# A two-layer RG-LRU and gated-DeltaNet trunk: one-step scaling of the decays, and further margins in the generator that writes the instruction order

## The chip, the cores and the metric

The kernel runs on one core of one Trainium2 chip. The metric is the device time of one launch in microseconds (us). A launch takes the host's arrays and returns the output; nothing is computed on the host.

The core has five engines that run side by side, each through its own list of instructions in the written order: TensorE (PE in the profile; PEld is its loading of weights), VectorE (DVE), ScalarE (ACT), GpSimd (POOL) and SyncE (SP). SyncE here only issues DMA transfers. An instruction that waits for a result holds everything behind it on its engine.

## The reference

The input x has 2048 frames of 1024 channels, all in float32. Layer 0 mixes with a recurrent block (RG-LRU), layer 1 with a gated delta rule (DeltaNet) of 8 heads of 128.

```python
c_act = jax.nn.silu(c)
for i in range(2):
    shift, scale, gate = split(c_act @ ada_w[i] + ada_b[i])
    h = rmsnorm(x, norm_g[i]) * (1.0 + scale) + shift
    out = rglru_block(h, ...) if i == 0 else gated_deltanet_block(h, ...)
    x = x + gate * out
return rmsnorm(x, final_g)

# rglru_block: proj = h @ in_w (1024 -> 2048); causal conv of width 4; two gates per 128-wide block;
#   h_t = a_t h_{t-1} + b_t over all frames; times SiLU(z); @ out_w (1024 -> 1024)
# gated_deltanet_block: proj = h @ in_w (1024 -> 4096 + 16); causal conv and SiLU on q, k, v; l2norm of q, k;
#   per head, in chunks:
#     S_t = a_t S_{t-1} + beta_t k_t (v_t - a_t S_{t-1}^T k_t)^T,   o_t = S_t^T q_t
#   rmsnorm per head, times SiLU(z), @ out_w (1024 -> 1024)
```

## The kernel before

The frames are taken in two halves of 1024 (`u`), each in two pieces of 512 (`i`). The program runs through these stages: projections of layer 0 for u = 0 and 1 ("in1"), the output projection of layer 0 ("out1"), projections and heads of layer 1 for u = 0 and 1 ("in2"), the output projection of layer 1 with the last norm ("out2"). Every large product is done as three matmuls in a reduced float32 format, hi x hi, hi x lo and lo x hi, so each weight and each activation is split: ScalarE or VectorE makes the hi copy, and VectorE or GpSimd subtracts it to get lo. Such a 128x512 product is line L668 in the profile; its tile is `mm` in the projections and `mmo` in the output projections.

For layer 1, each of the 32 column panels of a half (k, v, q and z of 8 heads) has its weights split as it comes: `whi` by ScalarE (L644) and `wlo` by GpSimd (L650, 128x1024). In the second half `wlo` is loaded back from memory and GpSimd doesn't compute it again. A k, v or q panel goes through `conv2_thread`: a copy, three taps on VectorE (L718), a tanh on ScalarE (`tt`, L1009), and a product on VectorE (`kt`, `vt`, `qt`, L1014).

Per head and piece, `key_thread` makes the decay matrix `ec` (128 x 4 x 128: four blocks of 128 frames), gets `cc` (one number per row and block) from GpSimd, scales `ec` by it (L1162), and multiplies it with k k^T (`ac`). `inverses_thread` inverts the 32x32 corners in 31 steps on VectorE (`ttmp`, `tblk`, L1293 and L1296); `levels_thread` builds the inverse of 128x128 from them (`px`, `pr`). `recurrence_thread` then takes eight blocks in a row: `pp` (state times k and q, TensorE), `zt` (VectorE, L1422), `py` (TensorE), `yt` (ScalarE, L1436), `pS` (TensorE), the new `state` (VectorE, L1455). `output_thread` adds the two parts of the output and takes its square (`junko`).

No order is written by hand. The functions are generators ("threads"), and at build time a planner, `Weave`, runs them in a model time. A thread yields what it needs next: `"act", 0.53` is 0.53 us on ScalarE (an optional third number is the delay until others see the result), `"none", 0.5` is a pause that occupies no engine, an `Event` is a result of another thread, and `Slots` are the buffers of a ring. The planner always resumes the thread that can start first, and the code behind the yield then emits its instructions. So the model times set the order in each engine's list; they issue nothing. Waits between engines come from the data.

Two rings matter here. `raw` has two buffers of 4 KB per partition; the weight panels, the `ada_w` pieces, the pieces of the output weights (`oraw`) and the first eight rows `ot` of the last norm share it. `xr` has two buffers, shared by the lo parts `xl` of the gates in layer 0 and the residual pieces of out1.

In `out_weights_thread` the output weights come in pieces of 512 KB (L896); `out_split_thread` makes their `oh` (ScalarE, L907) and `ol` (VectorE, L909). The residual pieces are loaded in L970 and stored in L959, the product of the layer goes out in L849, and the kept lo weights in L658.

## Time and profile before

| | |
|---|---|
| median of 3 runs | 1942.98 us (1942.18 to 1945.73) |
| profiled execution | 1942.17 us, its span 1940.5 us, mean TensorE clock 0.984 |
| instructions in the profile | 31373 |
| TensorE matmuls in the profile | 10286, busy 1846.8 us |
| VectorE, ScalarE, GpSimd busy | 1479.8, 1045.5, 647.4 us |
| memory traffic | 322.77 MB, mean 166 GB/s |

All durations in the text come from that one profiled execution. A row of a group of instructions has the line, the engine, the operation, the tiles written and read, the shapes and the count, and then the busy time in us, the mean of one in ns, and the idle time of the engine just before them with what ended it. A row for a line's spread has minimum, median and maximum in ns. A row of the chain of waits has who waited for whom, the total in us, the count and the longest. A row of a timeline has the start and the duration in us; in brackets stands the idle time before it. A row of windows has, for each engine, the busy time and the count, and then the granted TensorE clock (1.00 is full), the DMA share and GB/s.

### The profile page before, as it was taken

The numbers are of one execution on the slowest core, as the hardware profiler recorded it, in microseconds if no ns is written. First come the engines' busy times: TensorE is split into PE (matmuls) and PEld (weight loads), VectorE is DVE, ScalarE is ACT, GpSimd is POOL, SyncE is SP. The second block draws the span as 40 slices with busy tenths as digits, with TensorE's granted clock in tenths as the row PEclk, the third lists the DMA queues.
The fourth block names the chain that finished last, engine by engine and source line by source line (L and its number), as shares of the span: only waits on it lengthen the run. The fifth ranks groups of instructions, "written<-read, shape, count | busy, mean of one in ns | idle before, by whom it ended". The sixth has DMA issues, their size and how long they took to land.

```text
span 1940.5 us, 31373 instructions
## 1 busy us (share of the span) xinstructions
PE 1846.8 (95%) x10286; PEld 1505.6 (78%) x10286; DVE 1479.8 (76%) x3271; ACT 1045.5 (54%) x2587; POOL 647.4 (33%) x1116
## 2 busy tenths in 40 slices
PE   6999899999899998998999999999999999999998
PEld 3787678878687777787777777787888888888887
DVE  6899998887454668869878987668787878886653
ACT  3766667667211345475565654565766656655221
POOL 3345542223100244345435532333333223301110
PEclk9999999999899999999999999999999999999999
DMA  8476746554578634556676645556465555586751
GB/s 319 114 221 190 225 140 220 182 161 139 168 209 223 206 110 136 139 136 159 156 180 156 141 119 168 144 136 169 105 159 152 149 127 144 143 233 201 246 160 66
DMA packets 511724, 322.77 MB, mean 166 GB/s; under 512 B 371268, under 2 KB 439236, under 8 KB 511560
## 3 DMA queue, kind: packets, MB, share of 16 engines
q1 hardware_dynamic: 511560, 320.77, 58.7%
q8 instruction: 81, 1.33, 0.3%
q14 instruction: 83, 0.68, 0.1%
HBM read 219.93 MB, written 100.73 MB: 165 GB/s over the span
## 4 chain that ended last, share of the span: by engine, by line
PE 51%; DVE 22%; DMA 10%; ACT 6%; issue 4%; SPq 4%; POOL 2%; DVEq 0%; POOLq 0%; ACTq 0%
PE mm L668 25%; PE mmo L668 15%; DVE xf L718 4%; DVE ttmp L1293 2%; DVE tblk L1296 2%; PE pg L807 2%; DMA blk<-blk_d 1%; DMA raw<-in_w 1%; DMA ada<-in_ada_w 1%; DVE xf L756 1%; PE pp L1413 1%; PE pS L1442 1%; PE py L1430 1%; PE pS L1443 1%; ACT junk L1146 1%
## 5 line engine op out<-in xcount | busy, mean ns | idle before, releaser
L718 DVE SCALAR_TENSOR_TENSOR xf<-xe,cw_s,xf 128x512 f32<-128x512 f32 x288 | 231.0, 806 | 20.3 <-POOL xf L997 16.3
L650 POOL TENSOR_TENSOR wlo<-raw,whi 128x1024 fp32r<-128x1024 f32 x48 | 119.4, 2487 | 141.6 <-ACT whi L644 132.1
L1293 DVE TENSOR_TENSOR ttmp<-blk,tblk 128x60 f32<-128x60 f32 (+24 forms) x496 | 122.4, 247 | 15.7 <-DMA blk<-blk_d 6.6
L644 ACT CAST whi<-raw 128x1024 fp32r<-128x1024 f32 x96 | 100.0, 1042 | 59.1 <-DMA raw<-in_w 51.9
L1296 DVE TENSOR_TENSOR tblk<-tblk,ttmp 128x60 f32<-128x60 f32 (+24 forms) x496 | 121.8, 246 | 10.4 <-DVE ttmp L1293 0.9
L668 PE MATMUL mmo<-oh,yh 128*128 128x512 f32 x256 | 102.1, 399 | 5.0 <-ACT oh L907 5.0
L668 PE MATMUL mm<-hh_('in2', 0)_5342,whi 128*128 128x512 f32 x256 | 105.6, 413 | 0.8 <-ACT xe L730 0.8
L668 PE MATMUL mm<-hh_('in2', 0)_5437,wlo 128*128 128x512 f32 x256 | 105.3, 411 | 0.0
L668 PE MATMUL mmo<-ol,yh 128*128 128x512 f32 x256 | 102.4, 400 | 3.0 <-DVE ol L909 3.0
L668 PE MATMUL mm<-hh_('in2', 1)_12057,whi 128*128 128x512 f32 x256 | 104.9, 410 | 0.0
L668 PE MATMUL mm<-hl_('in2', 0)_5438,whi 128*128 128x512 f32 x256 | 104.9, 410 | 0.0
L668 PE MATMUL mm<-hh_('in2', 0)_5437,whi 128*128 128x512 f32 x256 | 104.7, 409 | 0.0
L668 PE MATMUL mm<-hh_('in2', 1)_12057,wlo 128*128 128x512 f32 x256 | 104.5, 408 | 0.0
L668 PE MATMUL mm<-hl_('in2', 0)_5343,whi 128*128 128x512 f32 x256 | 104.1, 407 | 0.0
L668 PE MATMUL mm<-hl_('in2', 1)_12307,whi 128*128 128x512 f32 x256 | 103.9, 406 | 0.0
L668 PE MATMUL mm<-hh_('in2', 0)_5342,wlo 128*128 128x512 f32 x256 | 103.7, 405 | 0.0
L668 PE MATMUL mm<-hh_('in2', 1)_12306,wlo 128*128 128x512 f32 x256 | 103.5, 404 | 0.0
L668 PE MATMUL mm<-hl_('in2', 1)_12058,whi 128*128 128x512 f32 x256 | 103.5, 404 | 0.0
L668 PE MATMUL mm<-hh_('in2', 1)_12306,whi 128*128 128x512 f32 x256 | 103.4, 404 | 0.0
L668 PE MATMUL mmo<-ol,oh 128*128 128x512 f32 (+1 forms) x264 | 103.0, 390 | 0.0
L668 PE MATMUL mmo<-oh,ol 128*128 128x512 f32 (+1 forms) x264 | 102.9, 390 | 0.0
L668 PE MATMUL mmo<-oh,yl 128*128 128x512 f32 x256 | 102.1, 399 | 0.5 <-DVE yl L929 0.5
(331 smaller groups left out, 5651.9 us busy)
## 6 DMA issues: line engine op xcount, KB each, us to landing
raw<-in_w SPq DMA_DIRECT2D x96, 512.0 KB, 4.2
araw<-in_ada_w SPq DMA_DIRECT2D x32, 512.0 KB, 4.2
xt<-x_d SPq DMA_DIRECT2D x32, 512.0 KB, 4.7
xt_d<-xb SPq DMA_DIRECT2D x192, 64.0 KB, 2.4
xk<-xt_d SPq DMA_DIRECT2D x24, 512.0 KB, 6.2
xt<-in_x SPq DMA_DIRECT2D x16, 512.0 KB, 4.5
ada<-in_ada_w SPq DMA_DIRECT2D x16, 512.0 KB, 8.8
y_d<-tz SPq DMA_DIRECT2D x32, 256.0 KB, 3.1
```

The source lines that it names most:

```text
L644: act.copy(hi, raw)
L650: pool.tensor_tensor(lo, raw, f(hi), ALU.subtract)
L668: pe.matmul(pt, lhsT=lhs[a][:, k, :], rhs=rhs[b][:, k, :], start=(k == 0 and n == 0), stop=(k == KT - 1 and n == 2))
L718: dve.scalar_tensor_tensor(xf, xe[:, 1 + j:1 + j + TC], wc[:, j:j + 1], xf, ALU.mult, ALU.add)
L756: dve.scalar_tensor_tensor(xf[:, 3:TC], pt[:, j:j + TC - 3], wc[:, j:j + 1], xf[:, 3:TC], ALU.mult, ALU.add)
L807: pe.matmul(pg, lhsT=a[:, g, :], rhs=b, start=(q == 0), stop=(q == 2))
L1146: act.activation(junk, kd[:, b, :], AF.Square, accum_out=ss[:, b:b + 1])
L1293: dve.tensor_tensor(tmp, blk[:, j, j + 1:32].unsqueeze(2).to_broadcast([P, r, c_]), t[:, j, 0:c_].unsqueeze(1).to_broadcast([P, r, c_]), A ...
L1296: dve.tensor_tensor(t[:, j + 1:32, 0:c_], t[:, j + 1:32, 0:c_], tmp, ALU.subtract)
L1413: pe.matmul(pp[:, 0, :], lhsT=kc, rhs=S_, start=True, stop=True)
L1430: pe.matmul(py, lhsT=rm[:, b, :], rhs=zt, start=True, stop=True)
L1442: pe.matmul(pS[:, 0, :], lhsT=kd[:, b, :], rhs=yt, start=True, stop=True)
```

## The change

The change has five parts.

1. `key_thread`: the four VectorE instructions that scale the blocks of `ec` become one `tensor_tensor` over all four, with `cc` broadcast along the row. The planner's cost goes from 4 x 0.14 to 0.62 with a delay of 0.13, and the delay behind GpSimd's `cc` from 0.2 to 0.7.
2. `out_split_thread`: a pause of 0.8 in the plan before the hi copy.
3. `conv2_thread`: a pause of 0.5 before the tanh, and a longer delay behind its product (0.5 for k, 1.0 for q, 0.3 for v instead of 0.3).
4. `output_thread`: a pause of 0.5 before the square.
5. `finish_thread`: before it takes a buffer for its row it waits for the event that the last output weights are issued.

```diff
     def out_split_thread(key, d, k, raw, rtok, scale, hi, lo, after):
         for e in after:
             yield e
+        yield "none", 0.8
         yield "act", 0.95
...
         put("xe", etok)
+        yield "none", 0.5
         yield "act", 0.53
         tt = tile_([P, TC], "tt", "tt")
         act.activation(tt, xf, AF.Tanh)
...
-        yield "dve", EV
+        yield "dve", EV, {"k": 0.5, "q": 1.0, "v": 0.3}[kind]
         r = tile_([P, TC], kind + "t", kind + "t")
...
-        yield "pool", 0.5
+        yield "pool", 0.5, 0.7
         pool.tensor_tensor(cc, rr, rr, ALU.mult)
         pool.tensor_tensor(cc, cc, beta[:, i * TB:(i + 1) * TB, h], ALU.mult)
-        for b in range(TB):
-            yield "dve", 0.14, 0.0
-            dve.tensor_scalar(ec[:, b, :], ec[:, b, :], cc[:, b:b + 1], None, ALU.mult)
+        yield "dve", 0.62, 0.13
+        dve.tensor_tensor(ec, ec, cc.unsqueeze(2).to_broadcast([P, TB, P]), ALU.mult)
...
             put("t2", ttok)
+            yield "none", 0.5
         rq = (yield ev("rq", u, h, m // TB))[0]
...
         otag = "raw" if b < AHEAD else "ot"
+        yield ev("owissue", 2, 1)
         otok = yield slots[otag]
```

The instructions are the same but for part 1 (128 `tensor_scalar` become 32 `tensor_tensor`) and for the table loads of ScalarE that the compiler puts in, which go from 53 to 47. The order is the same until the end of layer 0's second half, where the output weights are first split, and differs everywhere behind. Line numbers behind the first edit are one to three higher.

SyncE at the start of out1, before: `oraw` are the last four loads of output weights, `xr` the residual pieces, `raw` the first panels of layer 1, `x_d<-xr` and `y_d<-tz` stores.

```order
L896 DMA oraw<-in_ow 128x1024
L606 DMA raw_4163<-in_w 128x1024
L658 DMA wlo_d2k_4140<-wlo 128x1024
L970 DMA xr<-in_x 128x512 x2
L896 DMA oraw<-in_ow 128x1024 x2
L959 DMA x_d<-xr 128x512
L849 DMA y_d<-tz 128x512
L658 DMA wlo_d2v_4225<-wlo 128x1024
L970 DMA xr<-in_x 128x512
L959 DMA x_d<-xr 128x512
L970 DMA xr<-in_x 128x512
L896 DMA oraw<-in_ow 128x1024
```

The same place now:

```order
L896 DMA oraw<-in_ow 128x1024
L849 DMA y_d<-tz 128x512 x2
L971 DMA xr<-in_x 128x512
L606 DMA raw_4177<-in_w 128x1024
L896 DMA oraw<-in_ow 128x1024
L658 DMA wlo_d2k_4152<-wlo 128x1024
L971 DMA xr<-in_x 128x512
L896 DMA oraw<-in_ow 128x1024
L658 DMA wlo_d2v_4235<-wlo 128x1024
L960 DMA x_d<-xr 128x512
L896 DMA oraw<-in_ow 128x1024
L849 DMA y_d<-tz 128x512
```

The second to fourth loads of weights have moved up past residual loads and stores; the last `araw` load of layer 1's conditioning, which stood ahead of all this, now stands behind it.

VectorE at the first two pieces of the first head of layer 1, before:

```order
L1014 SCALAR_TENSOR_TENSOR qt<-tt,xf 128x512 x2
L1224 STREAM_TRANSPOSE tb<-qt 128x512 x2
L1162 TENSOR_SCALAR ec<-ec,cc 128x128 x8
L1025 SCALAR_TENSOR_TENSOR tz<-tz,mm 128x512
L1174 TENSOR_TENSOR ac<-pkk,ec 128x512
```

The same place now:

```order
L1016 SCALAR_TENSOR_TENSOR qt<-tt,xf 128x512 x2
L1225 STREAM_TRANSPOSE tb<-qt 128x512 x2
L1163 TENSOR_TENSOR ec<-ec,cc 128x512 x2
L1027 SCALAR_TENSOR_TENSOR tz<-tz,mm 128x512
L1175 TENSOR_TENSOR ac<-pkk,ec 128x512
```

Eight instructions have become two, and what stands around them is the same here.

TensorE at the fifth head (head 4) of layer 1's first half, where the inverse ends (`px`, `pr` of 64x64) and the recurrence of that head (`state_106`) begins, before; `mm` are projections of later heads:

```order
L1258 MATMUL pqk<-qt,kt 128x128 x2
L1364 MATMUL px_10222<-tf,ac 64x64 x8
L1258 MATMUL pqk<-qt,kt 128x128 x2
L668 MATMUL mm<-hh_('in2', 0)_5342,wlo 128x512
L668 MATMUL mm<-hh_('in2', 0)_5342,whi 128x512
L668 MATMUL mm<-hl_('in2', 0)_5343,whi 128x512
L668 MATMUL mm<-hh_('in2', 0)_5342,wlo 128x512
L668 MATMUL mm<-hh_('in2', 0)_5342,whi 128x512
L668 MATMUL mm<-hl_('in2', 0)_5343,whi 128x512
L668 MATMUL mm<-hh_('in2', 0)_5342,wlo 128x512
L1374 MATMUL pr_10262<-ac,tf 64x64 x8
```

The same place now:

```order
L668 MATMUL mm<-hh_('in2', 0)_5342,wlo 128x512
L1365 MATMUL px_10522<-tf,ac 64x64 x8
L1375 MATMUL pr_10546<-ac,tf 64x64 x8
L1431 MATMUL py<-vn,ac 128x128
L1443 MATMUL pS<-yt,kd 128x128
L1444 MATMUL pS<-yt,at 128x128
L1414 MATMUL pp<-state_106,kt 128x128
L1415 MATMUL pp<-state_106,qt 128x128
L1431 MATMUL py<-zt,ac 128x128
```

The projections that stood between `px` and `pr`, and between the steps of the recurrence, are gone from here for three steps; the inverse of this head begins 79 large matmuls later in TensorE's list than before.

## The prediction

> **What bounds the kernel now.** I read the page's engine totals first, then the span cut into the program's stages, then the chain of waits of TensorE, then the timelines around its largest gaps.
>
> ```profile
> PE 1846.8 (95%) x10286; PEld 1505.6 (78%) x10286; DVE 1479.8 (76%) x3271; ACT 1045.5 (54%) x2587; POOL 647.4 (33%) x1116
> ...
> core 0: us, PE busy (x) PEld busy (x) DVE busy (x) ACT busy (x) POOL busy (x), PEclk, DMA share, GB/s
> 485.00:640.00 155.00, 146.45 (x614) 117.10 (x613) 76.34 (x100) 32.95 (x41) 12.39 (x23) 0.97 0.71 201
> ...
> 727.00:1212.00 485.00, 448.60 (x2898) 369.39 (x2896) 407.09 (x1081) 273.82 (x851) 220.79 (x399) 0.97 0.59 149
> ...
> 1330.00:1750.00 420.00, 414.81 (x2857) 347.52 (x2856) 336.24 (x991) 254.16 (x798) 126.05 (x320) 1.00 0.60 155
> ```
>
> TensorE is busy 95%, and the change neither adds nor removes a matmul. So it can only move the idle time of TensorE and the time that its clock is halved after idle time. The stage cut says where they lie: the entry of the first output projection (485 to 640) has 155 - 146.45 = 8.5 us idle; the first half of the second layer (727 to 1212) has 485 - 448.60 = 36.4 us idle, and its mean clock of 0.97 is worth another 0.03 x 485 = 14.5 us at half speed; the second half (1330 to 1750) has 5 us and a full clock. Before about 440 us the order is the same in both programs, so the idle time there stays.
>
> In the stage with 36.4 us VectorE is busy 407 of 485 us, and TensorE's waits there name VectorE:
>
> ```profile
> PE pp L1413 <- DVE state L1455: 5.2, 6, 1.7
> PE py L1430 <- DVE zt L1422: 3.9, 4, 1.8
> PE pk L1135 <- DVE tblk L1296: 3.8, 2, 2.3
> PE pqk L1258 <- DVE qt L1014: 3.2, 2, 3.0
> ```
>
> The columns are the total, the count and the longest. The waits are many and short, spread over several products of VectorE: VectorE falls behind the written order in bursts, and TensorE pays.
>
> **The out_split margin (0.8 before the hi copy) and what it moves.** The one large idle stretch with a single cause is at the start of the first output projection. TensorE's timeline, the SyncE queue's, one ScalarE row, and the window:
>
> ```profile
> 488.36 0.39 PE L668 MATMUL mmo<-ol,yh 128*128 128x512 f32 x1
> 488.59 0.39 PE L668 MATMUL mmo<-oh,yl 128*128 128x512 f32 x1
> 492.83 0.51 PE L668 MATMUL mmo<-oh,yh 128*128 128x512 f32 x1 [3.85 <-ACT oh L907]
> 495.58 0.80 PE L668 MATMUL mmo<-ol,yh 128*128 128x512 f32 x1 [2.24 <-DVE ol L909]
> 496.17 0.63 PE L668 MATMUL mmo<-oh,yl 128*128 128x512 f32 x1
> ...
> 500.01 0.63 PE L668 MATMUL mmo<-oh,yl 128*128 128x512 f32 x1
> 501.80 0.51 PE L668 MATMUL mmo<-oh,yh 128*128 128x512 f32 x1 [1.16 <-ACT oh L907]
> 503.06 0.50 PE L668 MATMUL mmo<-ol,yh 128*128 128x512 f32 x1 [0.76 <-DVE ol L909]
> ...
> 475.02 7.80 SPq L970 DMA_DIRECT2D xr<-in_x  x2
> 482.92 0.89 SPq L896 DMA_DIRECT2D oraw<-in_ow  x2
> 495.56 0.38 SPq L896 DMA_DIRECT2D oraw<-in_ow  x1
> ...
> 500.69 1.06 ACT L907 ACTIVATE oh<-oraw 128x1024 fp32r<-128x1024 f32 x1 [5.03 <-DMA oraw<-in_ow]
> ...
> 488.90:503.80 14.90, 6.88 (x17) 0.77 0.65 223
> 503.80:520.00 16.20, 16.20 (x64) 0.89 0.44 142
> ```
>
> TensorE loses 3.85 + 2.24 + 1.16 + 0.76 = 8.0 us. Between 496.17 and 500.01 there are nine steps of 0.427 us, where the step before the gap is 0.23 (488.36 to 488.59); 12 such matmuls cost 12 x 0.19 = 2.3 us more, and the 16.2 us behind them, at a clock of 0.89, another 0.11 x 16.2 = 1.8. I price the place at 8.0 + 2.3 + 1.8 = 12 us. Its cause is SyncE: two loads of weights stand behind two xr loads that hold the queue for 7.8 us, and the fourth load is issued only at 495.56, after three stores and loads of the residual. In the new order the four weight loads stand apart: the second follows one xr load only, the fourth stands ahead of the y_d store and the third xr load, where it stood behind both and another xr load. Counting from the second xr load, which now waits for a gate product that ends 8 + 6 matmuls into the projection where it was 27 + 6, the third load can go some 19 x 0.23 = 4.4 us earlier. ScalarE's hi copies then come in time for the first three pairs; the fourth still waits for a raw buffer (a lo copy, the issue, 5 us to landing as in the ScalarE row, hi, lo), and I estimate 3 us of gap left in two pieces, too short for a long clock drop. Term: -9. Ends: -12 (all of it) and +2 (an ada load and its product now stand inside the projection, behind those loads, and TensorE waits for that product in its order). ScalarE also loses six table loads (53 to 47 in the order); it is busy 54%, so they hide beside TensorE and cost or bring nothing, also if that cover goes, since they are fewer.
>
> **One-step scaling.** Four tensor_scalar of 128x128 become one tensor_tensor of 128x512, 32 times, and cc is now a broadcast second input.
>
> ```profile
> L1162 DVE TENSOR_SCALAR ec<-ec,cc 128x128 f32<-128x128 f32 x128 | 41.0, 363 | 12.1 <-POOL cc L1159 11.8
> 984.61 0.88 DVE L1162 TENSOR_SCALAR ec<-ec,cc 128x128 f32<-128x128 f32 x4 [0.53 <-POOL cc L1159]
> L834 DVE TENSOR_TENSOR tg<-tg x32: 674/683/2817, 80.4 to 497.7; 128x512 f32<-128x512 f32 x32
> L408 DVE TENSOR_SCALAR acc<-araw,c_col x8: 473/476/1139, 116.9 to 432.8; 128x512 f32<-128x512 f32 x8
> ...
> 1146.73 2.39 POOL L650 TENSOR_TENSOR wlo<-raw,whi 128x1024 fp32r<-128x1024 f32 x1 [0.21 <-ACT whi L644]
> 1146.81 2.43 DVE L1162 TENSOR_SCALAR ec<-ec,cc 128x128 f32<-128x128 f32 x1
> 1152.16 0.46 PE L1413 MATMUL pp<-state,kt 128*128 128x128 f32 x2 [2.22 <-DVE tblk L1296]
> 1167.36 3.12 DVE L1162 TENSOR_SCALAR ec<-ec,cc 128x128 f32<-128x128 f32 x4
> 1176.42 1.49 PE L1335 MATMUL px<-tf,ac 32*32 32x32 f32 x32 [2.11 <-DVE tz L1025]
> ```
>
> Undisturbed, four take 0.88 us end to end; the nearest row for the new form, a tensor_tensor of the same shape with both inputs in SBUF, has a median of 0.683. That frees 0.2 x 32 = 6 us of VectorE, 3 of them in the tight stage. The mean is worse than the clean four: 41.0 / 32 = 1.28 us, because some of the 128 are held for the length of GpSimd's 2.4 us lo subtraction (the rows at 1146.81 and in 1167.36). Behind those two holds stand two TensorE gaps, 2.22 and 2.11 us. One instruction offers GpSimd one place to slip in ahead, not four. I take one of the two gaps as gone with a clock loss like the entry's 2.3 us behind it: 2.1 + 2.3, rounded to -4. Ends: -12 (both gaps, 4.3, their clock losses, 4.6, and 3 us of VectorE) and +4 (one 0.68 us block now sits inside the inverse chain where four short ones filled its latencies).
>
> A rule speaks against this edit. The Trainium skill, "VectorE: DVE Perf Modes", section "Mode 2×_2P — use both read ports for one tensor", says that an fp32 tensor_scalar can run at two results a cycle and a tensor_tensor only at one. By it, an estimate from that page, 512 elements would go from 0.27 to 0.53 us, VectorE would pay 8.5 us more, and the sum would be about 1937. The long rows agree with it (0.473 against 0.683 us at 512 elements), the clean group of four does not: its four starts cost more than the rate saves.
>
> **The other margins** (0.5 before tanh; 0.5, 1.0, 0.3 behind it; 0.5 ahead of the output's square; 0.7 behind GpSimd's cc) issue nothing. They tell the generator that these results come later, so that it writes other work ahead of them.
>
> ```profile
> ACT tt L1009 <- DVE xf L718: 74.3, 43, 6.0
> ACT junko L1479 <- DVE oo L1473: 73.9, 61, 4.1
> DVE qt L1014 <- ACT tt L1009: 13.4, 7, 5.2
> ...
> L1422 DVE SCALAR_TENSOR_TENSOR zt<-pp,eg,vn x120: 302/346/354, 817.2 to 1790.5; 128x128 f32<-128x128 f32 x120
> L1436 ACT ACTIVATE yt<-py x128: 252/278/291, 814.5 to 1791.8; 128x128 f32<-128x128 f32 x128
> L1455 DVE SCALAR_TENSOR_TENSOR state<-state,eg,pS x112: 294/346/351, 820.0 to 1788.9; 128x128 f32<-128x128 f32 x112
> ```
>
> ScalarE stands 74 us before the tanh with everything behind it held, and VectorE waits 13.4 us for the tanh of q; the TensorE wait behind that one was 3.2 us in the tight stage. These are the waits that the margins address. TensorE's VectorE waits quoted above sum to 16.1 us there; I take a third, -5. Ends: -15 (nearly all) and +10, since any new order draws new collisions with GpSimd's subtractions, which are not in the generator's model.
>
> **A new bare stretch.** In the new order the inverse of head 4 stands 79 large matmuls later (18 us of TensorE), and behind it TensorE has three steps of the recurrence with no projection matmul between them, where before each had four or five. Each bare step waits for 0.346 + 0.278 + 0.346 = 0.97 us of VectorE and ScalarE: 2.9 us; two copies of the inverse, taken at 0.35 each like these rows, 0.7; and a clock loss like the entry's, 2.3. Term: +6. Ends: 0 (before had gaps of its own around there) and +16 (the inverse is later still than written).
>
> **The raw rows.** finish_thread now waits until the output weights are issued. In both orders all eight loads stand ahead of the first use of such a row, so nothing moves: 0. What would be late without it is not in this order.
>
> **Sum.** The profiled execution took 1942.17 us (span 1940.5); -9 -4 -5 +6 = -12 gives 1930.2. The median of the runs is 0.8 us above that execution, so 1931.
>
> **Rivals.**
> *The hold stays.* GpSimd's 2.4 us subtraction holds the new tensor_tensor as it held the old ones; L834's maximum of 2817 ns shows that such an instruction is held too. The scaling then brings nothing: 1935. The Trainium skill, "SBUF — State Buffer", section "Who interferes with whom", states that a VectorE instruction with two SBUF inputs contends with a GpSimd one that reads SBUF; the L834 row agrees. Chance 0.13, and 0.03 for the dearer form by L408's rate (0.21 x 32 = 6.7 us of VectorE, half of it felt): 1938.
> *A trade.* The tight stage draws as many new collisions as it sheds, the margins come out at +5 instead of -5, and with the entry's -9 the rest cancels: 1941 to 1945, no change that can be told (a measurement tells 0.2%, 3.9 us, from nothing). For it speaks that VectorE's bursts come from GpSimd, which the edits don't touch. Chance 0.18.
> *Slower: head 4's inverse.* If that inverse is later than written, the rings of k and q are full, no projection matmul can stand in, and every microsecond passes to TensorE, with the clock loss on top. From 18 us of loss there instead of 6 the change is nothing; at 30 us, a lateness as long again as the 18 us that the order shows, it is 1955. Against it: the longest waits for state and zt before were 1.7 and 1.8 us. Chance 0.16.
>
> **Numbers.** The forecast has 0.50, with its own range 1921 to 1938. Faster: 0.50 + 0.13 + 0.03 and nothing of the rest, 0.66; same 0.18; slower 0.16. The range that keeps 8 in 10 runs from 1919 (the entry and both holds gone, margins at -12) to 1947.
>
> **What would show it.** Right: the gaps at L668's oh and ol near 490 shrink from 8.0 us to some 3 with a window clock over 0.9; the ec group has 32 instructions of about 0.7 us, under 30 us in all; the 727 to 1212 stage has under 33 us idle; a run of pp, py, pS gaps of 0.3 to 1 us near 980. Wrong: an entry that still loses over 8 us, more than 40 us idle in the first half of layer two, or gaps of over 3 us ahead of head 4's px.

## The result, and the profile after

| | median | range | ratio to before, 95% interval |
|---|---|---|---|
| before | 1944.36 us, 6 runs | 1937.58 to 1950.06 | |
| after | 1961.38 us, 6 runs | 1956.26 to 1963.69 | 1.0076 [1.0057, 1.0096] |

The change makes the kernel 0.76% slower, some 15 us by the ratio (the two medians are 17 us apart), where 1931 us was forecast. Of all the runs in this document one, of fill_head4, took 2289 us at a mean clock of 0.75, and it is left out of that kernel's ratio. The profiled execution of after took 1960.88 us, its span 1959.2 us, its mean clock 0.971 (0.984 before). First the engine totals of after:

```profile
PE 1852.6 (95%) x10286; PEld 1517.1 (77%) x10286; DVE 1460.8 (75%) x3175; ACT 1045.0 (53%) x2581; POOL 657.1 (34%) x1116
```

Then its windows, with the columns of those shown of before:

```profile
485.00:640.00 155.00, 148.97 (x633) 119.39 (x632) 78.15 (x103) 30.91 (x38) 12.55 (x22) 0.98 0.72 200
488.90:503.80 14.90, 9.40 (x34) 6.74 (x33) 10.65 (x12) 4.65 (x6) 4.63 (x5) 0.82 0.58 202
727.00:1212.00 485.00, 437.78 (x2711) 363.20 (x2710) 380.03 (x980) 264.66 (x822) 219.37 (x396) 0.94 0.58 144
```

VectorE has less to do (1460.8 us for 1479.8) and the entry of out1 is busier (9.40 us of 14.9 for 6.88). But in the first half of layer two TensorE is idle 485 - 437.78 = 47.2 us where it was 36.4, and the clock there is 0.94 where it was 0.97. The loss is in that stage alone. The starts of the large matmuls (L668, 6168 in each kernel, in the same sequence; numbered from 0) show where; each number is read off TensorE's timeline:

```
large matmul no.              1536   2304   3520    3584    3776    3840    5376    6144
start before, us             474.8  667.2  1091.8  1111.3  1189.9  1217.3  1739.6  1930.5
start after, us              478.2  666.6  1091.8  1136.6  1200.9  1245.2  1758.3  1949.2
after minus before            +3.4   -0.6    0.0   +25.3   +11.0   +27.9   +18.7   +18.7
```

Such a start differs by some us between single executions: one_step_old_order (below), whose plan is that of before, has +2.2 at 1536 too. Out1 (1536 to 2304) gains 4 us. At 3520 the two kernels are level, but after has 116 small TensorE instructions (two to a matmul) fewer behind it: head 4's recurrence begins at large matmul 3433 in before and at 3528 in after. So head 4's place lies behind 3520: 25.3 us are lost by 3584, where after does 200 of them and before 44, and 14.3 come back by 3776, where it is 172 and 292; 11 are left, with 36 of them more done than in before. From 3776 to the end of the half (3840) another 16.9 us go; 9.2 come back in the second half. TensorE's waits in after from 727 to 1245 us, the longest groups (total, count, longest), name the second place:

```profile
PE px L1336 <- DVE tz L1027: 13.5, 1, 13.5
PE pk L1137 <- DVE kt L1016: 5.8, 1, 5.8
PE px L1336 <- DVE tf L1329: 4.1, 4, 1.9
PE pk L1137 <- DVE tblk L1297: 4.0, 2, 2.8
```

Head 4's place, TensorE's timeline of after, in which no projection stands between the steps:

```profile
1093.76 1.14 PE L1365 MATMUL px<-tf,ac 64*64 64x64 f32 x16
1095.37 0.67 PE L1375 MATMUL pr<-ac,tf 64*64 64x64 f32 x8 [0.47 <-ACT tf L1367]
1097.49 0.67 PE L1375 MATMUL pr<-ac,tf 64*64 64x64 f32 x8 [1.45 <-DVE tf L1369]
1099.59 0.80 PE L1431 MATMUL py<-vn,ac 128*128 128x128 f32 x2 [1.42 <-DVE ac L1378]
...
1104.03 0.80 PE L1431 MATMUL py<-zt,ac 128*128 128x128 f32 x2 [0.44 <-DVE zt L1423]
1105.19 0.80 PE L1443 MATMUL pS<-yt,kd 128*128 128x128 f32 x2 [0.37 <-ACT yt L1437]
...
1108.53 0.80 PE L1431 MATMUL py<-zt,ac 128*128 128x128 f32 x2 [0.44 <-DVE zt L1423]
...
1112.24 0.77 PE L668 MATMUL mm<-hh_('in2', 0)_5437,whi 128*128 128x512 f32 x1
```

Two windows of after, one inside this place and one at the second place, which comes next:

```profile
1099.50:1116.00 16.50, 13.16 (x40) 10.12 (x41) 12.08 (x43) 6.00 (x19) 1.44 (x1) 0.50 0.29 50
1209.00:1228.50 19.50, 9.38 (x93) 7.49 (x94) 11.87 (x47) 6.74 (x17) 4.36 (x7) 0.50 0.60 199
```

A bare step takes 1108.53 - 1104.03 = 4.5 us, all at a clock of 0.50. The waits in it look small (0.44, 0.37, 0.44), since TensorE counts as busy while its own matmuls run, here at half clock.

The second place, 48 large matmuls ahead of the half's end, in the timelines of TensorE, VectorE, ScalarE and SyncE:

```profile
1218.19 1.73 PE L1336 MATMUL px<-tf,ac 32*32 32x32 f32 x32 [13.51 <-DVE tz L1027]
...
1199.07 0.19 DVE L1294 TENSOR_TENSOR ttmp<-blk,tblk 128x31 f32<-128x31 f32 x1 [3.27 <-POOL tblk L1288]
1213.41 0.43 DVE L569 CAST hh_('in2', 1)_11895<-h 128x512 fp32r<-128x512 f32 x1 [3.59 <-ACT h L561]
1217.45 0.68 DVE L1027 SCALAR_TENSOR_TENSOR tz<-tz,mm 128x512 f32<-128x512 f32 x1
...
1212.56 0.82 ACT L561 ACTIVATE h<-xk,cond 128x512 f32<-128x512 f32 x1 [4.52 <-issue]
1216.41 0.60 ACT L1025 ACTIVATE tz<-mm 128x512 f32<-128x512 f32 x1 [3.04 <-DMA z_d<-tz]
...
1202.79 2.73 SPq L1230 DMA_DIRECT2D q_d<-tb  x4
...
1206.20 1.88 SPq L546 DMA_DIRECT2D xk<-xt_d  x3
1208.13 1.08 SPq L1030 DMA_DIRECT2D z_d<-tz  x2
```

This `px` belongs to head 6. It needs one of two PSUM buffers that it shares with the gate products `z`, and is held until `tz` (a gate's last step) has read one. On ScalarE that `tz` stands behind the first `h` of the second half's input, whose load SyncE issued at 1206.20, and then waits 3.04 us more, until 1216.41, for the store of an earlier `tz`, which SyncE issued at 1208.13 behind those loads. On VectorE it stands behind most of head 7's inverse, which began late behind GpSimd, and behind the first split (`hh`); there it starts 0.44 us after ScalarE's part has ended (1217.01). So in this execution it is mainly that store that holds it. TensorE waits 13.5 us; in the second window above, which begins inside the wait, the clock is at 0.50 throughout.

### The profile page after: what moved, and what is told of

The parts are those of the page before. It is cut to its first block, busy times and chain, and to the rows that moved or that the text cites. A ratio compares the mean times of both kernels' runs of the same rounds, so it can differ in the third digit from the quotient of the medians.

```text
span 1959.2 us, 31257 instructions
## 1 busy us (share of the span) xinstructions
PE 1852.6 (95%) x10286; PEld 1517.1 (77%) x10286; DVE 1460.8 (75%) x3175; ACT 1045.0 (53%) x2581; POOL 657.1 (34%) x1116
## 4 chain that ended last, share of the span: by engine, by line
PE 62%; DVE 17%; DMA 8%; ACT 5%; issue 4%; SPq 3%; POOL 1%; DVEq 0%; POOLq 0%; ACTq 0%
PE mm L668 33%; PE mmo L668 15%; DVE tblk L1297 2%; DVE xf L718 2%; DVE ttmp L1294 2%; PE py L1431 1%; PE pp L1414 1%; PE pg L807 1%; PE pS L1443 1%; PE pS L1444 1%; PE pp L1415 1%; DMA raw<-in_w 1%; DMA ada<-in_ada_w 1%; PE pqk L1259 1%; PE pkk L1171 1%
## 5 line engine op out<-in xcount | busy, mean ns | idle before, releaser
L1297 DVE TENSOR_TENSOR tblk<-tblk,ttmp 128x60 f32<-128x60 f32 (+24 forms) x496 | 129.2, 261 | 11.0 <-POOL tblk L1288 0.3
L1294 DVE TENSOR_TENSOR ttmp<-blk,tblk 128x60 f32<-128x60 f32 (+24 forms) x496 | 117.2, 236 | 17.2 <-POOL tblk L1288 3.3
L668 PE MATMUL mm<-hh_('in2', 0)_5437,whi 128*128 128x512 f32 x256 | 108.7, 424 | 3.1 <-DVE tf L1369 2.2
L668 PE MATMUL mm<-hl_('in2', 0)_5438,whi 128*128 128x512 f32 x256 | 108.1, 422 | 0.0
L668 PE MATMUL mm<-hh_('in2', 0)_5437,wlo 128*128 128x512 f32 x256 | 107.3, 419 | 0.0
L668 PE MATMUL mmo<-ol,yh 128*128 128x512 f32 x256 | 101.7, 397 | 4.6 <-DVE ol L910 4.5
L668 PE MATMUL mm<-hh_('in2', 0)_5342,whi 128*128 128x512 f32 x256 | 104.2, 407 | 1.2 <-ACT tz L1025 1.2
L668 PE MATMUL mm<-hh_('in2', 1)_12191,wlo 128*128 128x512 f32 x256 | 104.7, 409 | 0.0
L668 PE MATMUL mm<-hl_('in2', 1)_12192,whi 128*128 128x512 f32 x256 | 104.3, 407 | 0.0
L668 PE MATMUL mm<-hh_('in2', 1)_11895,wlo 128*128 128x512 f32 x256 | 104.1, 407 | 0.0
L668 PE MATMUL mm<-hl_('in2', 0)_5343,whi 128*128 128x512 f32 x256 | 103.7, 405 | 0.0
L668 PE MATMUL mm<-hh_('in2', 1)_11895,whi 128*128 128x512 f32 x256 | 103.4, 404 | 0.1
L668 PE MATMUL mm<-hh_('in2', 0)_5342,wlo 128*128 128x512 f32 x256 | 103.4, 404 | 0.0
L668 PE MATMUL mm<-hl_('in2', 1)_11896,whi 128*128 128x512 f32 x256 | 103.3, 403 | 0.0
L668 PE MATMUL mm<-hh_('in2', 1)_12191,whi 128*128 128x512 f32 x256 | 103.2, 403 | 0.0
L668 PE MATMUL mmo<-oh,oh 128*128 128x512 f32 (+1 forms) x264 | 103.1, 390 | 0.0
L668 PE MATMUL mmo<-ol,oh 128*128 128x512 f32 (+1 forms) x264 | 102.8, 389 | 0.0
L668 PE MATMUL mmo<-oh,ol 128*128 128x512 f32 (+1 forms) x264 | 102.6, 389 | 0.0
L668 PE MATMUL mmo<-oh,yh 128*128 128x512 f32 x256 | 101.3, 396 | 0.9 <-ACT oh L908 0.9
```

The lines of the kernel that those rows point to most:

```text
L668: pe.matmul(pt, lhsT=lhs[a][:, k, :], rhs=rhs[b][:, k, :], start=(k == 0 and n == 0), stop=(k == KT - 1 and n == 2))
L1294: dve.tensor_tensor(tmp, blk[:, j, j + 1:32].unsqueeze(2).to_broadcast([P, r, c_]), t[:, j, 0:c_].unsqueeze(1).to_broadcast([P, r, c_]), A ...
L1297: dve.tensor_tensor(t[:, j + 1:32, 0:c_], t[:, j + 1:32, 0:c_], tmp, ALU.subtract)
```

## The experiments

Ratios are to the kernel before on the same chip, with 95% intervals; "the good pair" is the kernel before with the one-step instruction and the pause of part 2. Theory A, from the traces: the order of layer two's first half loses the time, not the new instruction. Rival B: the instruction does.

**The instruction, the pause and the new order taken apart.** The planner's costs and the instruction can be changed apart from each other, and part 2 leaves the order of layer two's heads as it is (out1 and the entry of out2 change).

```diff
# one_step_old_order: before, the plan untouched
         for b in range(TB):
             yield "dve", 0.14, 0.0
-            dve.tensor_scalar(ec[:, b, :], ec[:, b, :], cc[:, b:b + 1], None, ALU.mult)
+        dve.tensor_tensor(ec, ec, cc.unsqueeze(2).to_broadcast([P, TB, P]), ALU.mult)
# four_step_new_order: after, the four tensor_scalar behind  yield "dve", 0.62, 0.13
# one_step_and_pause: one_step_old_order, and  yield "none", 0.8  in out_split_thread
# all_but_pause: after without that pause
```

> The kernel before with the one-step tensor_tensor alone; the plan's costs are left as they were, so every other instruction stands where it stood. Theory A (the loss comes from the new order of layer 1's first half, not from the instruction): -6 to 0 us against before, ratio 0.997 to 1.000; the ec group 32 instructions of about 0.69 us. Rival B (the instruction itself loses: held by GpSimd or sitting inside the inverse's chain): +5 us or more, ratio over 1.0025, with new TensorE waits behind ec.

> The changed kernel with the four 128x128 tensor_scalar in place of the one instruction, under the same planner's costs, so in the changed kernel's order. Theory A: as slow as the changed kernel or up to 6 us slower, ratio to before 1.007 to 1.012; the bare stretch of head 4 and the 13 us gap at the end of the first half are both there. Rival B: most of the loss is gone, ratio 0.998 to 1.003.

> The kernel before with the one-step instruction (old costs) and the pause of 0.8 before the hi copy of the output weights; layer 1's first half keeps the order of before. Theory A: the entry of out1 gains and nothing is lost behind it: 4 to 9 us faster than the one-step instruction in the old order, ratio to before 0.993 to 0.998. Rival (what the entry gains is given back by the end of out1, where TensorE is then held by the next layer's first panels): within 2 us of the one-step instruction in the old order.

> The changed kernel without the pause of 0.8: out1 has the order of before, layer 1 that of the changed kernel. Theory A: 4 to 9 us slower than the changed kernel, ratio to before 1.009 to 1.013, the whole loss in layer 1's first half. Rival (the entry's gain is given back by the end of out1): same as the changed kernel within 2 us, ratio 1.006 to 1.009.

| | ratio | median us | before, same chip |
|---|---|---|---|
| one_step_old_order | 0.9966 [0.9949, 0.9982] | 1939.29 | 1944.66 |
| four_step_new_order | 1.0088 [1.0069, 1.0107] | 1962.47 | |
| one_step_and_pause | 0.9938 [0.9917, 0.9958] | 1934.13 | |
| all_but_pause | 1.0096 [1.0078, 1.0115] | 1965.14 | |

A holds on the first three and B falls; on all_but_pause the interval reaches from A's range into that of its rival (the entry's gain is given back by the end of out1), so it says no more than that the kernel is some 2 to 4 us slower than the changed one. With the order kept, the instruction gains 6.6 us (0.0034 x 1944.66). With the old four instructions in the new order the loss is all there. The pause gains 5.4 us more (0.9966 to 0.9938; with the later 0.9952 it is 2.7), so parts 1 and 2, without the new planner's costs, make a kernel faster than both. How the one-step form does it, from one_step_old_order. The spread of its instruction (minimum, median, maximum in ns):

```profile
L1162 DVE TENSOR_TENSOR ec<-ec,cc x32: 647/692/1099, 724.9 to 1685.7; 128x512 f32<-128x512 f32 x32
```

The timelines of the same kernel where the prediction saw the two holds, of VectorE, GpSimd and TensorE:

```profile
1142.97 2.41 DVE L1296 TENSOR_TENSOR tblk<-tblk,ttmp 128x42 f32<-128x42 f32 x1
1145.31 0.68 DVE L1162 TENSOR_TENSOR ec<-ec,cc 128x512 f32<-128x512 f32 x1
...
1142.95 2.38 POOL L650 TENSOR_TENSOR wlo<-raw,whi 128x1024 fp32r<-128x1024 f32 x1 [0.31 <-ACT whi L644]
...
1148.64 0.46 PE L1413 MATMUL pp<-state,kt 128*128 128x128 f32 x2 [2.49 <-DVE tblk L1296]
1170.41 1.09 PE L1335 MATMUL px<-tf,ac 32*32 32x32 f32 x32 [1.25 <-DVE tz L1025]
```

No scaling is held for 2.4 us any more, but here GpSimd's subtraction holds the neighbour `tblk` instead, and TensorE's gap behind it stays (2.49 us, before 2.22). The other gap, ahead of `px`, shrinks from 2.11 to 1.25.

**One margin at a time on the good pair.** Theory A1: bare steps are what costs, so they can be counted in an order ahead of time. A2: only the whole set harms. A3: the margins of conv2_thread do it.

```diff
# add_scaling_costs:   yield "pool", 0.5, 0.7   and   yield "dve", 0.62, 0.13
# add_conv_margins:    yield "none", 0.5 before the tanh; {"k": 0.5, "q": 1.0, "v": 0.3} behind the product
# add_square_pause:    yield "none", 0.5 before the square
# all three with finish_thread's wait as well
# one_step_and_pause_2 (later, on another chip): the good pair and finish_thread's wait
```

> The faster version (one-step instruction and pause, 0.994 of before) with one more edit of the change, the planner's new costs for the scaling (0.62 with 0.13, and 0.7 behind cc). Theory A1 (a bare stretch of the recurrence is what costs, wherever it falls): this order has three steps bare after large matmul 2856 and four after 3858 in layer 1's first half, so 8 to 16 us are lost against the faster version: ratio 0.998 to 1.003. Rival A2 (the loss comes with the whole set of margins, a single one is harmless): 0.992 to 0.996.

> The faster version with the margins of conv2_thread (0.5 before the tanh; 0.5, 1.0, 0.3 behind the product). Theory A1: this order has no bare stretch of three steps in layer 1's first half, so within 4 us of the faster version, ratio 0.992 to 0.996. Rival A3 (these margins move the heads behind the projections and make the gap at the end of the first half): 10 us or more lost, ratio 0.999 or more, with a gap of over 8 us ahead of head 7's px.

> The faster version with the pause of 0.5 ahead of the output's square. Theory A1: no bare stretch in this order, so within 4 us of the faster version, ratio 0.992 to 0.996. Rival A2 agrees; a ratio over 0.999 would put the loss on this pause.

> The faster version once more, with finish_thread's wait written in, which changes no instruction, no wait and no order. Part 5 of the change as forecast: nothing, ratio 0.992 to 0.996 as the faster version had. If the wait did cost something by itself: over 0.998.

Measured: 1.0067 [1.0045, 1.0090], 1.0041 [1.0023, 1.0059], 1.0007 [0.9993, 1.0022], and the good pair again 0.9952 [0.9934, 0.9971]. Each margin alone takes away what the pair had won, and more in two of three. In their traces add_square_pause has no bare step, and add_conv_margins two in a row, not three; both lose. So A1 isn't enough, and A2 falls. A3's sign isn't there: the longest gap of add_conv_margins is 4.6 us, ahead of a `pk`, and the end of its first half comes earlier than in before (large matmul 3840 at 1211.4 us for 1217.3). So no one margin is the culprit. The wait in finish_thread costs nothing that can be told, as forecast.

**The clock at head 4.** Matmuls of `ident` by `ident` fill the waits of the bare stretch.

```diff
+                for _ in range(6 if b == 0 else 2):
+                    pe.matmul(py, lhsT=ident, rhs=ident, start=True, stop=True)
# the same ahead of pS and pp of these steps, and 6 ahead of the second pr
```

> The changed kernel with 37 matmuls of ident by ident (128x128, some 0.21 us each at full clock) put into the bare stretch of head 4 in the first half, written into tiles that the real matmuls then overwrite: 8 ahead of waits for the second pr and 28 or so ahead of py, pS and pp of the first three steps. They do no useful work; all else stands as in the changed kernel. Clock theory (the halved clock of 17 us comes from the idle time and doubles TensorE's part of each step): the granted clock there is 1.0 or close to it, the three steps take some 3 us each in place of 4.5, and the kernel is 5 to 9 us faster than the changed one, ratio to before 1.003 to 1.006. Rival (the waits for VectorE and ScalarE set the step, the clock costs little): no gain or up to 4 us slower, ratio 1.007 to 1.010.

(The trace has 28 such matmuls, not 37: 6, 10, 6 and 6 ahead of pr, py, pS and pp.) 1.0081 [1.0050, 1.0111]: no gain that can be told over the changed kernel. Two of its TensorE rows, one step apart:

```profile
1098.00 0.49 PE L1441 MATMUL py<-zt,ac 128*128 128x128 f32 x2 [0.22 <-DVE zt L1429]
...
1101.42 0.49 PE L1441 MATMUL py<-zt,ac 128*128 128x128 f32 x2
```

The window around them:

```profile
1090.00:1108.00 18.00, 15.32 (x109) 12.99 (x108) 15.86 (x54) 8.16 (x26) 3.90 (x7) 1.00 0.36 78
```

The clock is full (1.00 where it was 0.50), but the step still takes 1101.42 - 1098.00 = 3.42 us. Against the changed kernel the place gains 2.5 us (matmul 3584 is 9.3 us earlier, 3520 already 6.8). The useless matmuls may lengthen this step, since the `py` at 1101.42 stands right behind two of them without a wait. The trace of add_scaling_costs has a bare step at a full clock without them, two rows of TensorE and the window between:

```profile
1227.84 0.49 PE L1413 MATMUL pp<-state,kt 128*128 128x128 f32 x2 [0.44 <-DVE state L1455]
...
1231.01 0.49 PE L1413 MATMUL pp<-state,kt 128*128 128x128 f32 x2 [0.44 <-DVE state L1455]
...
1227.84:1231.01 3.17, 1.91 (x11) 1.34 (x11) 0.90 (x4) 2.99 (x9) 0.00 (x0) 1.00 0.68 176
```

That step takes 3.17 us. So idle time did halve the clock, which is worth some 1.3 us of the 4.5 in a step, but the chain of dependent results makes most of the price. The clock theory was near with its step of 3 us and wrong with the 5 to 9 us for the kernel.

**The 13 us gap.** The queue theory: SyncE issues late. The order theory: `tz` stands behind the next half's split on two in-order engines. (The first of the three texts, like that of add_conv_margins, calls the `px` head 7's; it is head 6's.)

```diff
# next_half_by_pool, for the first three loads:
-            sp.dma_start(out=xk, ...)
+            pool.dma_start(out=xk, ...)
# gates_first: after's order, with
#   SyncE:   xk x3 behind z_d x2 (was ahead)
#   ScalarE: the first h behind one tanh of a gate
#   VectorE: the first hh and hl behind one tz
# changed_again: after itself, on the chip of gates_first
```

> The changed kernel, where the first three loads of the second half's input (xk) are issued by GpSimd's queue in place of SyncE's; every other instruction stands as in the changed kernel. Queue theory (the 13 us gap at the end of the first half comes from SyncE, whose queue has no break from 1188 to 1210 us, so that xk and the two z stores behind it are issued late): xk is issued near 1200 in place of 1206, the gap ahead of head 7's px shrinks from 13.5 to 7 to 9 us, and the kernel is 4 to 8 us faster than the changed one, ratio to before 1.0035 to 1.006. Rival (VectorE's and ScalarE's order, with the next half's split ahead of the last gates, sets the gap whatever the queue does): gap of 12 us or more, ratio 1.0065 to 1.009.

> The changed kernel with a local exchange at the 13 us gap near the end of the first half, all else in the changed kernel's order: on SyncE the three xk loads stand behind the two z stores in place of ahead of them, on ScalarE the first h stands behind one gate's tanh, on VectorE the first hh and hl of the next half stand behind one tz, which frees the bank that px waits for. (The px there is head 6's; the two texts ahead of this one call it head 7's.) Order theory (px waits for tz, and tz stands behind the next half's first split on two in-order engines): the gap of 13.5 us shrinks to 7 to 10 us, the kernel gains 4 to 7 us against the changed one. Rival (the inverse on VectorE and the DMAs that feed it set tz's time, as they did when the loads went by GpSimd's queue): the gap stays over 12 us, less than 2 us are gained.

> The changed kernel again, as the base of the two beside it on the same chip: ratio to before 1.0057 to 1.0096, its interval so far; a gap of 13 to 14 us ahead of head 6's px and 17 to 20 us of halved clock behind each of the two bad places.

Measured: 1.0078 [1.0057, 1.0099], 1.0081 [1.0062, 1.0100] and 1.0084 [1.0061, 1.0106]. From the timelines of next_half_by_pool, TensorE at the place, GpSimd, SyncE and VectorE:

```profile
1217.94 1.72 PE L1336 MATMUL px<-tf,ac 32*32 32x32 f32 x32 [13.15 <-DVE tz L1027]
...
1199.67 2.45 POOL L546 DMA_DIRECT2D xk<-xt_d  x3
1203.28 5.10 SPq L1230 DMA_DIRECT2D q_d<-tb  x4
...
1208.16 0.30 DVE L1329 STREAM_TRANSPOSE tf<-ac 32x128 f32<-32x128 f32 x1 [2.69 <-DMA ac<-tt_d]
1217.21 0.68 DVE L1027 SCALAR_TENSOR_TENSOR tz<-tz,mm 128x512 f32<-128x512 f32 x1
```

TensorE at the place in gates_first:

```profile
1211.14 1.72 PE L1366 MATMUL px<-tf,ac 32*32 32x32 f32 x32 [9.34 <-DVE tz L1052]
```

And in changed_again:

```profile
1213.74 1.72 PE L1336 MATMUL px<-tf,ac 32*32 32x32 f32 x32 [12.88 <-DVE tz L1027]
```

The queue theory falls: the loads left 6.5 us earlier, but SyncE's stores of q took 5.10 us where they took 2.73, a load of `ac` for head 6's inverse came later (VectorE waits 2.69 us for it, 0.37 in after), and the gap stayed. There `tz` starts on VectorE at 1217.21 with no wait of its own, behind VectorE's other work. The order theory is right on the gap (12.88 to 9.34) and wrong on the gain: matmul 3840 starts at 1241.8 us, with changed_again at 1240.9, and from 3776 on both take some 43.8 us. What the exchange won at `px` was lost again in the 48 matmuls behind it. Since it moves the store ahead of the loads on SyncE and the order of ScalarE and VectorE together, it doesn't say which of them shortened the gap. What would free the matmuls behind `px` wasn't found.

**Size of a margin or draw of an order.** The pause ahead of the tanh gets other values in the changed kernel, and q's delay one.

```diff
-        yield "none", 0.5
+        yield "none", 0.45        # also 0.55, 0.3, 0.6, and without the line
         yield "act", 0.53
# q_margin_09: "q": 0.9 for 1.0
```

> The changed kernel with 0.45 in place of 0.5 as the pause ahead of the tanh in conv2_thread, nothing else. The order of layer 1's first half is another one again: no step of the recurrence stands bare, and head 7's px comes 29 large matmuls behind the end of the half in place of 5; the second half's order is much as it was. Draw theory (the margins' sizes don't matter, each value draws another order, and the change's values drew one with two bad places): 8 to 25 us faster than the changed kernel, ratio to before 0.995 to 1.004. Rival (further margins as such push the heads too late): within 5 us of the changed kernel, ratio 1.005 to 1.010.

> The changed kernel with 0.9 in place of 1.0 as the delay behind q's product, nothing else. This order has no bare steps either and head 7's px 30 large matmuls behind the end of the first half, but its second half is another one too. Draw theory: ratio to before 0.995 to 1.004, 8 to 25 us faster than the changed kernel. Rival (further margins as such): 1.005 to 1.010.

> The changed kernel with 0.55 in place of 0.5 as the pause ahead of the tanh, the other side of 0.45. Its order has three bare steps of the recurrence after large matmul 2852 and three after 3893, none at head 4, and head 7's px 21 large matmuls into the next half. Draw theory: another time again; bare steps cost 3 us or more each, so 6 to 20 us slower than with 0.45, ratio to before 0.996 to 1.004. Rival (the time rises steadily with the pause, from 0.993 at 0.45 through 1.0076 at 0.5): 1.010 or more.

> The changed kernel with 0.3 in place of 0.5 as the pause ahead of the tanh. Its order has the changed kernel's two features again, three bare steps at head 4 (after large matmul 3528) and head 6's px 48 large matmuls ahead of the end of the half, and three more bare steps after 3860. Draw theory (the place of these features in the order sets the time, not the pause): as slow as the changed kernel, ratio to before 1.004 to 1.012. Rival (the time rises with the pause: 0.993 at 0.45, 1.008 at 0.5, 1.011 at 0.55): 0.994 or less.

> The changed kernel with 0.6 as that pause. Its order has nothing bare at head 4 and head 6's px 99 large matmuls ahead of the end of the half, as in the kernel before; four bare steps after 3856. Draw theory: ratio to before 0.996 to 1.005, faster than with 0.5 and with 0.55. Rival (rises with the pause): 1.011 or more.

> The changed kernel without that pause, the longer delays behind the product kept. Its order has no bare steps, and head 6's px 112 large matmuls ahead of the end of the half. Draw theory: ratio to before 0.993 to 1.000. The rival gives 0.994 or less too, so a value over 0.997 speaks against the rival and one below tells nothing apart.

| pause | ratio | |
|---|---|---|
| none | 1.0094 [1.0066, 1.0121] | |
| 0.30 | 1.0130 [1.0104, 1.0155] | |
| 0.45 | 0.9933 [0.9914, 0.9951] | 1933.38 us, before 1945.58 |
| 0.50 | 1.0076 and 1.0084 | the change |
| 0.55 | 1.0110 [1.0090, 1.0129] | |
| 0.60 | 1.0017 [0.9999, 1.0036] | |
| 0.50, q 0.9 | 1.0023 [1.0008, 1.0038] | |

There is no trend: 0.05 us of model time, which issues nothing, is worth 28 us, and the size theory put 0.3 and 0.6 on the wrong sides. The draw theory forecast each time from features of the order. It was right with 0.60 and q 0.9, just outside its range with 0.45 and 0.30, and missed 0.55 (which came out where the rival had it) and the kernel without the pause. The traces show more than those two texts had read off the order: that of 0.55 has two bare steps behind large matmul 3528, head 4's place, and that of the kernel without the pause two behind 3672. And the forecasts give the second half no price. The starts of large matmuls, each less that of before:

```
large matmul no.          2304    3520    3584    3840    5376    6144
none, us                  -2.6    -3.8    -3.2    -0.5   +13.1   +14.5
0.45                      -1.3    -7.6   -10.8   -12.5   -11.2   -11.4
0.55                      -0.6   +10.8   +27.5   +17.6   +22.3   +26.1
0.50, q 0.9               -1.8    -5.0    -8.4   -13.7    +1.9    +7.3
```

Without the pause and with q 0.9 the first half loses nothing; the loss lies in the second (3840 to 5376). Its windows, without the pause and in before:

```profile
1216.84:1752.65 535.81, 520.82 (x3418) 433.17 (x3417) 409.30 (x1162) 318.13 (x982) 178.02 (x403) 0.98 0.57 149
1217.32:1739.58 522.26, 515.85 (x3438) 430.13 (x3437) 407.09 (x1188) 319.17 (x996) 170.03 (x406) 1.00 0.57 150
```

TensorE is idle there for 15.0 us (before 6.4), at a clock of 0.98. Which waits of these orders cost that wasn't followed up. So counting bare steps in the first half doesn't foretell an order's time; the chip has to. The window of 727 to 1212 us with 0.45:

```profile
727.00:1212.00 485.00, 450.14 (x2968) 373.12 (x2966) 397.83 (x1053) 285.93 (x887) 229.26 (x405) 0.99 0.62 154
```

The same window with 0.3:

```profile
727.00:1212.00 485.00, 444.22 (x2728) 367.80 (x2726) 383.02 (x979) 263.35 (x827) 219.78 (x395) 0.94 0.57 142
```

And TensorE's timeline with 0.3, at the two bad places:

```profile
1102.15 0.80 PE L1431 MATMUL py<-vn,ac 128*128 128x128 f32 x2 [7.02 <-DVE ac L1378]
...
1220.81 1.72 PE L1336 MATMUL px<-tf,ac 32*32 32x32 f32 x32 [10.47 <-DVE tz L1027]
```

With 0.45 TensorE does 2968 instructions in the stage where the change did 2711, at a clock of 0.99. With 0.3, where the order has the two places again, so has the trace. That place and loss go together in these two orders isn't proof: filling the waits of the one place and shortening the gap of the other didn't win the time back above.

## Why the prediction was wrong

**What bounds the kernel: right.** Neither matmuls nor another engine decided; TensorE's idle time and clock in the first half of layer two did.

**The entry of out1: right in kind, half the size.** -9 was forecast, and the pause is worth -5.4 or -2.7 by the two measurements of the good pair, -4 by the starts above. The loads stand apart and the gaps shrank from 8.0 us to 5.4, not to 3. Two are left, and the larger waits for the `ol` of the fourth load. SyncE issues that load at 490.56 and not at 495.56, and its `oh` is there at 496.4; but on VectorE the `ol` stands behind a product `acc` of layer 1's conditioning, which waits for its own load. The timelines of after, TensorE, SyncE and VectorE:

```profile
496.42 0.51 PE L668 MATMUL mmo<-oh,yh 128*128 128x512 f32 x1 [0.90 <-ACT oh L908]
501.38 0.79 PE L668 MATMUL mmo<-ol,yh 128*128 128x512 f32 x1 [4.46 <-DVE ol L910]
...
490.56 0.33 SPq L896 DMA_DIRECT2D oraw<-in_ow  x1
...
498.83 0.75 DVE L410 SCALAR_TENSOR_TENSOR acc<-araw,c_col,acc 128x512 f32<-128x512 f32 x1 [3.61 <-DMA araw<-in_ada_w]
...
500.11 1.22 DVE L910 SCALAR_TENSOR_TENSOR ol<-oraw,oh 128x1024 fp32r<-128x1024 f32 x1
```

This is the ada load that the prediction named as an end of its range, +2, and left out of the term: it holds VectorE for 3.61 us.

**One-step scaling: right in number, in part by luck.** -4 was forecast, -6.6 measured, inside the ends. 32 instructions of 0.69 us came out as priced, and VectorE lost 7.5 us of work in the old order (1479.8 to 1472.3). But the term took one of the two gaps as gone with its clock loss; one stayed (2.49 us) and the other shrank by 0.9. In the profiled execution large matmul 3328 already starts 4.2 us earlier (1019.9 for 1024.1), ahead of both; where the rest of the 6.6 us comes from isn't shown. The 8.5 us more of VectorE that the prediction estimated from the Trainium skill, "VectorE: DVE Perf Modes", section "Mode 2×_2P — use both read ports for one tensor", didn't come: the trace disagrees with the estimate, since four short instructions pay four starts, 0.2 us apart. (With half of them felt, as in the rival, that estimate would have given 1939 and not 1937.) The rival "the hold stays" was right on one gap of two: the hold passed to a neighbour. The Trainium skill, "SBUF — State Buffer", section "Who interferes with whom", calls the port pair that VectorE and GpSimd share an exclusive lock; the 2.41 us of `tblk` beside the 2.38 of GpSimd's subtraction agree, and say that it is whichever VectorE instruction stands there that pays.

**The other margins: the step that failed.** The prediction added up TensorE's waits for VectorE, 16.1 us, and took "a third, -5", with ends of -15 and +10. That prices margins as a cure for the waits that they name. They don't act on those: they redraw the order of the whole layer, and the new order has other waits. Together with the bare stretch the order was forecast at -5 + 6 = +1. From the good pair (0.9938 and 0.9952) to the changed kernel (1.0076 and 1.0084) it cost 24 to 28 us. Ten redrawn orders of layer two were measured here; one is as fast as the order of before (0.9933 beside 0.9938 and 0.9952), nine are slower, by 0.6 to 1.9 points. The order of before was among the best of its kind, so the end of +10 was far too near, and the middle should have lain above zero. What in each of these orders costs the time is open but for the two places of the changed kernel.

**The new bare stretch: seen, and mis-sized.** +6 was forecast, for three steps at 2.9 us, the inverse's copies at 0.7 and a clock loss of 2.3. In after the three steps take 12.65 us (1099.59 to 1112.24), of which some 3.2 are TensorE's own issue at full clock (15 matmuls, 0.21 from start to start, as `pp` has at 1117.44 and 1117.65): 9.5 us for 2.9. The waits for the inverse are 0.47 + 1.45 + 1.42 = 3.3 us for 0.7. The net is smaller, since before had gaps of its own: by the starts it is some 11 us (25.3 - 14.3), in which a few more small matmuls were done. The step was priced at VectorE's and ScalarE's 0.97 us. It costs the whole loop of results: 4.5 us, and 3.17 at a full clock. Even there 2.2 us pass from the start of a matmul until its result can be taken or in going from engine to engine, and the sum had no term for that. The steps stand at 1099 to 1112, not near 980.

**The gap of 13.5 us near the end of the half: not in the prediction at all.** It read the order at three places and not here, where a `px` now stands ahead of the half's last products with both buffers taken.

**The raw rows: right**, 0. **The rivals:** the one of the slower side named head 4 and the price from which it decides, 18 us, but as lateness of the inverse; the signs of that, gaps of over 3 us ahead of head 4's `px`, aren't in the trace. The other sign named for a failure is there: more than 40 us idle in the first half of layer two (47.2). The trade, 1941 to 1945, had the mechanism, new collisions for old, and stopped 16 us short.

## What to carry to other kernels

Where a planner orders the work, an edit of its model times is a new draw of the whole order, and its price is the spread of draws (here 2% over six values of one pause), not the waits that it aims at. Nine of the ten draws here lost against the order at hand, so ask how good that one already is among its kind before forecasting a gain. Make the edits that keep the order first and measure them alone, then try several values of a margin on the chip and keep the best. And price a recurrence step without cover at its whole loop, TensorE's own results included.

## What was not expected of the hardware

Waits of no more than 1.45 us each brought the clock down at head 4. In after it falls at 1099.3 and comes back at 1116.3. Windows of TensorE alone (length, busy time and count, then the clock, the DMA share and GB/s) show what stood ahead of both:

```profile
1095.89:1099.30 3.41, 0.82 (x11) 1.00 0.40 157
...
1112.94:1116.35 3.41, 3.41 (x12) 0.50 0.38 65
```

The clock fell behind 3.41 us in which TensorE was busy for 0.82, and came back behind 3.41 us without idle time; in between it stayed at 0.50, with TensorE busy for most of each such stretch. The Trainium skill, "TensorE: Matmul & The Clock Gate", Part 1, "The HAM clock gate", has the clock fall after an idle window of some 3.4 us and come back after a busy one of that length. The trace agrees on the return; on the fall it says that the window need not be idle in one piece. How much busy time keeps the clock up wasn't worked out. The 28 matmuls without use, put into the waits, held it at 1.00, and that was worth 2.5 us only.
